# Attention scores as 64-row matmuls of two heads, and a listed order for TensorE, in a two-layer decoder trunk

## The chip, the cores and the metric

The kernel runs on one core of one Trainium2 chip. The metric is the time of one execution on the device in microseconds (us); lower is better. Before the change the median of three runs is 952.17 us (951.81 to 952.43). One execution was recorded by the hardware profiler; "the profile" and "the trace" mean that record. In it PE is TensorE's matmuls, PEld its weight loads, DVE VectorE, ACT ScalarE, POOL GpSimd and SP SyncE, which issues the DMAs.

## The reference

One sequence of 512 tokens, 1024 channels, goes through a pooling layer with its MLP, then an attention layer with its MLP. Keys and values are projected once, from the residual stream after the first layer. The attention has 16 heads of 64 channels:

```python
z = einsum('bhqd,bhkd->bhqk', q_blk, k_blk) / sqrt(64)      # strictly causal, s < t
log1m = where(mask, -softplus(z), 0)
excl = cumsum(log1m, reverse=True) - log1m                  # over the keys
a = where(mask, exp(log_sigmoid(z) + excl), 0)
o = einsum('bhqk,bhkd->bhqd', a, v_blk)
m = o.reshape(B, S, HD) @ w_o
x = x + rms_norm(m, mix_post_g)
```

In words: a weight is the sigmoid of its own score times the product of (1 − sigmoid) over the keys between it and the query. Everything is float32.

## The kernel before, in words

**Accuracy and products.** TensorE multiplies float32 in a rounded form (`F32R`). So operands are split: the high part is the value rounded by a copy on ACT, the low part the rest, by a subtraction on DVE. A full product is three matmuls, high x high, high x low and low x high (`mm3`, L300 to L302, and `up_block`, L708 to L712, for projections of q and k and the MLP's first matrix).

**Heads and pairs.** The 16 heads form 8 pairs. A projection gives one PSUM tile of 128 rows (partitions) x 512 tokens; its rows 0–63 are head 0 of the pair, rows 64–127 head 1. `queries_keys` (L931) makes from it, for each head `a` of the pair, operands of 128 rows: `k` holds the high part of the head's keys twice (own half and other half of the partitions), `kl` the low part in the own half and zeros in the other half (set once by POOL), `q` the high part of the queries in the own half and their low part in the other. With these, one matmul over 128 rows gives qh·kh + ql·kh, and a second one qh·kl (L991, L992): two products of 128 rows stand for the three of 64.

**Scores.** For a block `i` of 128 queries only the keys up to the block's end count: 128, 256, 384 or 512 of them. `scores` takes at least 256. Its results fill three PSUM banks per head: block 3, block 2, and blocks 1 and 0 together.

**Weights.** ACT takes two sigmoids of each bank: of −z (`against`, L1000) for the scan, and of z (`for_`, L1012). DVE runs one scan over all 1280 entries of a head (`scan`, L1016) and multiplies (`weigh`, L1022). The scan's result `e` has one buffer. Then TensorE transposes the weights (`turn`, L1035: 10 transposes a head, in three PSUM tiles), ACT and DVE split them (`high`, `low`, L1041, L1045), and `products` (L1052) multiplies them with the values; `out_low` and `out` (L1059, L1063) collect the pair's output.

**Values** are projected for four heads at a time (two pairs; `values`, L882), one block of 128 tokens after another, 24 matmuls of 256 columns each. A group holds two weight tiles until its last block is done. Output projections (`contract`, `projected`) follow in between.

**PSUM** is one pool of 8 banks of 128 x 512 float32; every score tile, projection, transpose tile and product takes one.

**Weights from memory.** The attention's weight matrices were split during the first MLP and written back in two parts (`kept`). Four slots in SBUF hold them; SP loads the next one when a slot comes free (`w<-kept`, L242).

**What orders the work.** `ATT_ORDER` lists the attention's steps. P is the q and k projections of a pair, S its scores and weights (up to `weigh`), T its transposes and their splits, A its products with the values, V a group of value projections with its token blocks, O an output projection, N and K the first transposes and the first half of the first key projection, E the last four pairs' output. Only up to the first P does `manual_schedule` fix TensorE's order as listed; behind that a planner orders all engines by its own model of their times. From the last step on, `END_ORDER` fixes the order of all engines by hand: there z is a score, x and y the two sigmoids, sc the scan, mu the weigh, T the transposes of the last pair, A, oc and od the products of the sixth and last pair, D and R loads, O, E, F and G output projections. In both lists the digits are a pair, a head, a block or a tile.

Of the kernel before, what the change touches and what calls it, by code (L numbers as in the profile page):

```python
# [10 lines left out]
F32 = mybir.dt.float32  # L11
F32R = mybir.dt.float32r
ACT = mybir.ActivationFunctionType
ALU = mybir.AluOpType

P = 128
# [16 lines left out]
TS = [slice(t * P, (t + 1) * P) for t in range(T)]  # L33
# [3 lines left out]
SEG = {3: (0, 512), 2: (512, 384), 1: (896, 256), 0: (1152, 128)}  # L37
# [20 lines left out]

ATT_ORDER = [
    (w[0], int(w[1]), [int(c) for c in w[2:]])  # L60
    for w in """V001 N2 K0 N3 V02 P0 V03 S0 P1 T0 V101 S1 A0 P2 T1 V123 A1 S2 P3 T2 O00123 A2 S3 P4 V201 T3 A3
    S4 P5 T4 V223 S5 A4 P6 V301 T5 S6 A5 V323 P7 T6 E1""".split()
]


# [5 lines left out]

END_ORDER = [
    (w if w.startswith("d7") else w.rstrip("0123456789"), [int(c) for c in w if c.isdigit() and not w.startswith("d7")])
    for w in """D6 R0 R1 z01 z00 x01 z02 x00 z11 x02 z12 y02 sc0 A60 y01 y00 x11 z10 oc60 A61 y11 x10 od60 E01 y10
    mu0 oc61 x12 E00 y12 od61 sc1 T00 hh6 T02 T01 ah00 O00 ah02 d7h ah01 O01 hl6 al02 F01 mu1 E11 ov01
    T11 al00 T10 ah11 al01 F11 ah10 al11 T12 A70 al10 ah12 d7l al12 ov00 A71 oc70 od70 O10 oc71 od71 F00
    ov10 hh7 O11 hl7 G01 ov11 G00 ev01 G11 ev00 s01 E10 ev11 s00 g01 s11 F10 V0 g00 G10 a01 O20 a00 S01
# [28 lines left out]
def trunk(ctx, tc, x, consts, grow, pw, wup, wdn, wq, wk, wv, wo, out):  # L106
    nc = tc.nc
    pool = lambda name, bufs=1, **kw: ctx.enter_context(tc.tile_pool(name=name, bufs=bufs, **kw))
# [10 lines left out]
    def name(s):  # L119
        uid[0] += 1  # L120
        return f"{s}{uid[0]}"

    def ps():
        return psum.tile([P, 512], F32, tag="ps", name=name("ps"))
# [29 lines left out]
    behind, latest = {}, {}  # L154
# [32 lines left out]
    def want(key, src, scaled=None):  # L187
        queue.append((key, src, scaled))
# [48 lines left out]
    def make():  # L237
        k, src, scaled = queue.pop(0)
        if k in kept:
            made[k] = place(k)  # L240
            for n, t in enumerate(made[k]):
                latest["sp"] = nc.sync.dma_start(t.bitcast(F32), kept[k][n])  # L242
            return
        made[k] = weight(src, place(k), scaled, dn_raw.pop(k, None))

    def fill(n=1):
        if gate[0]:
            behind.update(latest)
        for _ in range(n):
            if queue and len(made) < ahead and (queue[0][0][0] != "dn" or dn_pool[0]):  # L250
                make()
# [6 lines left out]
    for l in range(2):  # L258
        if l == 1:
            n = len(queue)  # L260
            for what, i, part in ATT_ORDER:
                if what == "V" and 0 in part:
                    for h in range(2):
                        want(("v", i, h), wv[i, h], gains(C_KV * KC + 4 * h, 4))
                elif what == "P":
                    want(("k", i), wk[i], gains(C_KV * KC, KC))
                    want(("q", i), wq[i], gains(C_MIX_PRE1 * KC, KC))
                elif what == "O" or what == "E":
                    for c in range(2 * i, 2 * i + 2 if what == "O" else PAIRS):
                        want(("o", c), wo[c])  # L270
            apart.extend(x for x in queue[n:] if x[0] not in [("o", c) for c in range(2)])

            queue[n - GRP : n + GRP] = queue[n : n + GRP] + queue[n - GRP : n]
        for j in range(NJ):
            want(("up", l, j), wup[l, j])
        for j in range(NJ - GRP, NJ):
            want(("dn", l, j), wdn[l, j])
# [442 lines left out]
    with tc.tile_pool(name="mix0", bufs=1, reuse_waits="tile") as mp:  # L720
# [29 lines left out]
        left, stats, ups, ys, own = {}, {}, {}, {}, {}  # L750
# [128 lines left out]
    with tc.tile_pool(name="att", bufs=1, reuse_waits="tile") as ap:  # L879
# [30 lines left out]
        def project(key):  # L910
            need(*range(T))
            if key in started:
                pq, w = started.pop(key)
                up_block(pq, w, slice(S // 2, S))
            else:
                pq = ps()
                up_block(pq, get(key), slice(0, S))
            return pq

        def qk_tile(tag):  # L920
            return ap.tile([P, S], F32R, tag=tag, name=name(tag))

        half = [slice(0, HD), slice(HD, P)]


        kls = [qk_tile(f"kl{a}") for a in range(2)]
        with tc.issue_after(latest["pool"].ins):
            for a in range(2):
                nc.gpsimd.memset(kls[a][half[1 - a], :].bitcast(F32), 0.0)

        def queries_keys(p):  # L931
            qs, ks = [], []
            pk = project(("k", p))
            for a in range(2):
                k, kl, own, other = qk_tile(f"k{a}"), kls[a], half[a], half[1 - a]
                nc.scalar.copy(k[own, :], pk[own, :])
                latest["act"] = nc.scalar.copy(k[other, :], pk[own, :])
                latest["dve"] = nc.vector.tensor_tensor(
                    out=kl[own, :], in0=pk[own, :], in1=k[own, :].bitcast(F32), op=ALU.subtract
                )  # L940
                ks.append(k)
            fill()
            pq = project(("q", p))
            for a in range(2):
                q, own, other = qk_tile(f"q{a}"), half[a], half[1 - a]
                latest["act"] = nc.scalar.copy(q[own, :], pq[own, :])
                latest["dve"] = nc.vector.tensor_tensor(
                    out=q[other, :], in0=pq[own, :], in1=q[own, :].bitcast(F32), op=ALU.subtract
                )
                qs.append(q)  # L950
            fill()
            return qs, ks

        begin = ap.tile([P, NSEG], mybir.dt.bfloat16, tag="begin", name="begin")
        us = [ap.tile([P, NSEG + 1], F32, tag=f"u{a}", name=f"u{a}") for a in range(2)]
        with tc.issue_after(latest["pool"].ins):
            nc.gpsimd.memset(begin, 0.0)  # L960
            for lo, n in SEG.values():
# [3 lines left out]
                    out=d, in_=d, pattern=[[-1, P + c]], base=c - 1, channel_multiplier=1,  # L965
# [6 lines left out]
        class Head:  # L972
# [9 lines left out]
                self.qk, self.p, self.a, self.u = qk, p, a, us[a]  # L982
                self.pz, self.pt, self.parts, self.to = {}, {}, {}, {}

            def scores(self, b):
                q, k, kl = self.qk[0][self.a], self.qk[1][self.a], kls[self.a]
                pz = self.pz[b] = ps()
                o = 0
                for i in self.SCORES[b][0]:
                    n = max(256, (i + 1) * P)  # L990
                    nc.tensor.matmul(pz[:, o : o + n], q[:, TS[i]], k[:, :n], start=True, stop=False)  # L991
                    nc.tensor.matmul(pz[:, o : o + n], q[:, TS[i]], kl[:, :n], start=False, stop=True)  # L992
                    o += n

            def against(self, b):
                tiles, at = self.SCORES[b]
# [64 lines left out]
            def out(self, o):  # L1061
                own = half[self.a]
                nc.vector.tensor_tensor(out=o[own, :], in0=self.po[half[0], :], in1=o[own, :], op=ALU.add)  # L1063

        def weights(p):
            hs = [Head(qk[p], p, a) for a in range(2)]
            for x in hs:
                for b in range(3):
                    x.scores(b)
                    x.against(b)  # L1070
                    x.for_(b)
                x.scan()
                x.weigh()
            return hs

        def transposed(hs):
# [25 lines left out]
        vs, os, wos, y = {}, {}, {}, y_tiles()  # L1102
# [6 lines left out]
        def end():  # L1109

            p, last = PAIRS - 2, PAIRS - 1
            heads[last] = [Head(qk[last], last, a) for a in range(2)]
            w = {c: get(("o", c)) for c in range(2, 6)}
            bank, o, ups, up, held = {}, {}, {}, {}, []
# [77 lines left out]
            def half_up(j):  # L1192
# [2 lines left out]

            last_heads = heads[last]
            steps = {
                "z": lambda a, b: last_heads[a].scores(b), "x": lambda a, b: last_heads[a].against(b),
                "y": lambda a, b: last_heads[a].for_(b), "sc": lambda a: last_heads[a].scan(),
                "mu": lambda a: last_heads[a].weigh(), "T": lambda a, b: last_heads[a].turn(b),  # L1200
                "ah": lambda a, b: last_heads[a].high(b), "al": lambda a, b: last_heads[a].low(b),
# [24 lines left out]
        qk, heads, gpost1 = {}, {}, None  # L1226

        def step(what, i, part):
            nonlocal gpost1
            if what == "V":  # L1230
                values(i, part)
            elif what == "N":
                need(i)
            elif what == "K":
                start(("k", i))
            elif what == "P":
                qk[i] = queries_keys(i)
                if i == PAIRS - 1:
                    until(("o", 5))
            elif what == "S":  # L1240
                gate[0] = True
                heads[i] = weights(i)
                fill()
            elif what == "T":
                transposed(heads[i])
                behind.update(latest)
            elif what == "A":
                mix_pair(i, vs[i // 2][1])
            elif what == "O" and part:
                out_proj(i, part)  # L1250
                if i == 0:
                    with tc.issue_after(latest["sp"].ins):
                        gpost1 = gain_row(R_MIX_POST1)

        first = [what for what, _, _ in ATT_ORDER].index("P") + 1
        with tc.manual_schedule(engines={mybir.EngineType.PE}):
            for x in ATT_ORDER[:first]:
                step(*x)
        for x in ATT_ORDER[first:-1]:
            step(*x)  # L1260
        end()


# [56 lines left out]
```

## Time and profile before

| | |
|---|---|
| runs | 951.81, 952.17, 952.43 us |
| the profiled execution | 952.24 us, of which span 950.5 us |
| TensorE busy | 940.9 us (99% of the span), 4758 matmuls |
| DVE, ACT busy | 707.9 and 577.8 us |
| TensorE's clock | 0.999 of full |
| the attention | about 362 to 611 us of the span |

A row of the order in time reads: start in us, length in us, engine, line, operation, output <- inputs, shape, count, and in brackets the idle time ahead of it with what ended it. A matmul's length contains its pipeline's depth and overlaps the next one, so the distance between starts is what it takes. A row that groups instructions by line has the count behind x, then busy us, mean ns of one, then idle time ahead of them and what ended it. A row of waits names who waited <- for whom, total us, times, longest. A row of a window has, behind the window and its length, the busy us and count of PE, PEld, DVE, ACT and POOL, then TensorE's clock, the DMA engines' share and GB/s.

### The profile page before, as it was taken

What the parts mean: (1) busy time and instruction counts of PE and PEld (TensorE: products, weight loads), DVE (VectorE), ACT (ScalarE), POOL (GpSimd) and SP (SyncE); (2) the same over time, 40 slices, a digit from 0 to 9 for tenths busy, and PEclk for the clock granted to TensorE, in tenths of its full rate; (3) what the DMA queues carried; (4) which work ended last, traced back from release to release, by engine and by line L of the source; (5) the groups of instructions that cost most, each with busy time, mean ns of one, the idle gap of its engine ahead of it and who ended that gap; (6) DMA issues with size and microseconds to landing.
All of it is one profiled execution on the core that took longest, in us unless ns stands there. A gap on an engine that the chain in (4) does not pass through costs nothing.

```text
span 950.5 us, 12510 instructions
## 1 busy us (share of the span) xinstructions
PE 940.9 (99%) x4758; PEld 799.7 (84%) x4758; DVE 707.9 (74%) x813; ACT 577.8 (61%) x1015; POOL 42.1 (4%) x85
## 2 busy tenths in 40 slices
PE   9999999999999999999999999999999999999996
PEld 7998888888888889899899988898888888888885
DVE  5875798988979976476577778874696966958756
ACT  6667979788775547456656554865545444444532
POOL 2300000000000004000000000200000000000002
PEclk9999999999999999999999999999999999999999
DMA  8244969789697760522424271442513233133102
GB/s 309 96 178 148 342 219 347 295 283 356 217 323 269 271 207 2 202 85 90 172 95 178 91 264 45 134 155 71 196 43 131 93 133 111 45 133 111 35 11 89
DMA packets 43262, 156.15 MB, mean 164 GB/s; under 512 B 4289, under 2 KB 4673, under 8 KB 43202
## 3 DMA queue, kind: packets, MB, share of 16 engines
q1 hardware_dynamic: 43202, 155.36, 46.1%
q8 instruction: 37, 0.61, 0.3%
q14 instruction: 23, 0.19, 0.1%
HBM read 121.79 MB, written 33.55 MB: 163 GB/s over the span
## 4 chain that ended last, share of the span: by engine, by line
PE 94%; DVE 2%; ACT 2%; POOL 1%; issue 1%; POOLq 0%; DVEq 0%; ACTq 0%
PE ps L589 28%; PE ps L708 15%; PE ps L712 15%; PE ps L711 15%; PE ps L300 4%; PE ps L301 4%; PE ps L302 4%; PE ps L1052 2%; PE ps L829 1%; PE ps L1035 1%; PE ps L991 1%; PE ps L395 1%; PE ps L992 1%; ACT xn L285 1%; PE ps L801 1%
## 5 line engine op out<-in xcount | busy, mean ns | idle before, releaser
L589 PE MATMUL ps<-w,a 128*128 128x512 f32 x1176 | 278.6, 389 | 0.0
L711 PE MATMUL ps<-xnh,w 128*128 128x512 f32 (+1 forms) x712 | 261.1, 369 | 0.0
L712 PE MATMUL ps<-xnl,w 128*128 128x512 f32 (+1 forms) x712 | 261.1, 368 | 0.0
L708 PE MATMUL ps<-xnh,w 128*128 128x512 f32 (+1 forms) x712 | 260.3, 368 | 0.1
L589 PEld LDWEIGHTS ps<-w,a 128*128 128x128 f32 x1176 | 220.7, 188 | 45.9 <-DVE w L282 0.2
L712 PEld LDWEIGHTS ps<-xnl,w 128*128 128x128 f32 x712 | 134.2, 189 | 21.8
L708 PEld LDWEIGHTS ps<-xnh,w 128*128 128x128 f32 x712 | 133.7, 189 | 22.4 <-DVE w L850 0.3
L711 PEld LDWEIGHTS ps<-xnh,w 128*128 128x128 f32 x712 | 133.8, 189 | 22.1
L598 DVE TENSOR_TENSOR y<-ps,y 128x512 f32<-128x512 f32 x124 | 84.5, 688 | 43.9 <-PE ps L589 43.7
L172 DVE TENSOR_TENSOR w<-raw,w 128x1024 fp32r<-128x1024 f32 x58 | 70.9, 1223 | 57.4 <-ACT w L170 57.2
L170 ACT CAST w<-raw 128x1024 fp32r<-128x1024 f32 x58 | 61.0, 1051 | 79.3 <-PE ps L708 79.2
L281 ACT CAST a<-r 128x768 fp32r<-128x768 f32 (+1 forms) x60 | 47.7, 794 | 72.1 <-PE ps L589 55.7
L282 DVE TENSOR_TENSOR a<-r,a 128x768 fp32r<-128x768 f32 (+1 forms) x60 | 54.1, 902 | 12.3 <-ACT a L281 12.1
L281 ACT CAST w<-e 128x1536 fp32r<-128x1536 f32 (+1 forms) x30 | 41.8, 1394 | 23.8 <-DVE e L563 14.4
L1016 DVE TENSOR_TENSOR_SCAN e<-u,begin 128x1280 f32<-128x1280 f32 x16 | 45.2, 2823 | 11.0 <-ACT u L1000 10.4
L282 DVE TENSOR_TENSOR w<-e,w 128x1536 fp32r<-128x1536 f32 (+1 forms) x30 | 49.5, 1649 | 1.8 <-ACT w L281 1.6
L181 ACT ACTIVATE apart<-apart,eye 128x128 f32<-128x128 f32 (+1 forms) x132 | 43.1, 407 | 0.5 <-DMA apart<-in_wk 0.5
L282 DVE TENSOR_TENSOR w<-w,w 128x1536 fp32r<-128x1536 f32 (+1 forms) x20 | 33.0, 1650 | 8.6 <-ACT w L281 8.6
L621 ACT ACTIVATE r<-ps 128x512 f32<-128x512 f32 x56 | 33.1, 591 | 8.6 <-PE ps L708 8.5
L282 DVE TENSOR_TENSOR w<-xn,w 128x1536 fp32r<-128x1536 f32 (+1 forms) x20 | 33.0, 1650 | 5.6 <-ACT w L281 5.5
L300 PE MATMUL ps<-w,xnh 128*128 128x256 f32 x128 | 36.6, 286 | 0.0
L622 ACT ACTIVATE r<-r 128x512 f32<-128x512 f32 x56 | 35.5, 634 | 1.3
(134 smaller groups left out, 1393.6 us busy)
## 6 DMA issues: line engine op xcount, KB each, us to landing
raw<-in_wup SPq DMA_DIRECT2D x64, 512.0 KB, 4.1
w<-kept SPq DMA_DIRECT2D x60, 512.0 KB, 4.2
kept<-wx SPq DMA_DIRECT2D x30, 512.0 KB, 5.0
w<-in_wdn SPq DMA_DIRECT2D x8, 1536.0 KB, 6.7
kept<-apart SPq DMA_DIRECT2D x24, 512.0 KB, 5.7
xn<-in_wdn SPq DMA_DIRECT2D x8, 1536.0 KB, 7.7
apart<-in_wk SPq DMA_DIRECT2D x7, 512.0 KB, 7.1
apart<-in_wq SPq DMA_DIRECT2D x7, 512.0 KB, 9.4
```

The source lines that it names most:

```text
L170: nc.scalar.copy(hi, raw)
L172: nc.vector.tensor_tensor(out=lo, in0=raw, in1=hi.bitcast(F32), op=ALU.subtract)
L181: nc.scalar.mul(c, c, gc[:, lo + k : lo + k + 1])
L281: latest["act"] = nc.scalar.copy(hi, src)
L282: latest["dve"] = nc.vector.tensor_tensor(out=lo, in0=src, in1=hi.bitcast(F32), op=ALU.subtract)
L300: nc.tensor.matmul(dst, ah, bh, start=start, stop=False)
L589: nc.tensor.matmul(bank, a[:, x, q, TS[t]], w[:, z, q], start=start and q == 0 and k == 0, stop=q == self.n - 1 and k == 2, skip_group_che ...
L598: nc.vector.tensor_tensor(out=part, in0=bank, in1=part, op=ALU.add)
L708: nc.tensor.matmul(pu[:, cols], wl[:, k, :], xnh[:, k, cols], start=False, stop=k == KC - 1)
L711: nc.tensor.matmul(pu[:, cols], wh[:, k, :], xnh[:, k, cols], start=k == 0, stop=False)
L712: nc.tensor.matmul(pu[:, cols], wh[:, k, :], xnl[:, k, cols], start=False, stop=False)
L1016: nc.vector.tensor_tensor_scan(out=self.e[:, ::-1], data0=self.u[:, 1:][:, ::-1], data1=begin[:, ::-1], initial=0.0, op0=ALU.mult, op1=ALU ...
```

## The change

The pair's keys and queries are kept as they come from the projection: one high and one low tile of 128 rows each, head 0 in the upper and head 1 in the lower half. The scores of a head are three matmuls over its own 64 rows, and the two heads' matmuls alternate, each into a bank of its own. The shortest block takes 128 columns and no longer 256. Copies and zeros that built the 128-row operands go. In `weights` all scores of a pair come first, then the sigmoids of −z of both heads, then the first head's scan, then the sigmoids of z. TensorE's order of the whole attention up to the last step is the listed one, and the list has the value projections one token block at a time where they were mostly two at a time; in the last part the six score steps of two heads become three of the pair, ahead of the sixth pair's products.

```diff
-    for w in """V001 N2 K0 N3 V02 P0 V03 S0 P1 T0 V101 S1 A0 P2 T1 V123 A1 S2 P3 T2 O00123 A2 S3 P4 V201 T3 A3
-    S4 P5 T4 V223 S5 A4 P6 V301 T5 S6 A5 V323 P7 T6 E1""".split()
+    for w in """V001 N2 K0 N3 V02 P0 V03 S0 P1 V10 T0 V11 S1 A0 P2 T1 V12 A1 V13 S2 P3 T2 O00123 A2 S3 P4 V201 T3 S4
+    A3 P5 V22 T4 V23 S5 A4 P6 V30 T5 V31 S6 A5 V323 P7 T6 E1""".split()
...
-    for w in """D6 R0 R1 z01 z00 x01 z02 x00 z11 x02 z12 y02 sc0 A60 y01 y00 x11 z10 oc60 A61 y11 x10 od60 E01 y10
+    for w in """D6 R0 R1 z1 z0 x01 z2 x00 x02 y02 sc0 A60 y01 y00 x11 oc60 A61 y11 x10 od60 E01 y10
...
-        kls = [qk_tile(f"kl{a}") for a in range(2)]
-        with tc.issue_after(latest["pool"].ins):
-            for a in range(2):
-                nc.gpsimd.memset(kls[a][half[1 - a], :].bitcast(F32), 0.0)
-
         def queries_keys(p):
-            qs, ks = [], []
-            pk = project(("k", p))
-            for a in range(2):
-                k, kl, own, other = qk_tile(f"k{a}"), kls[a], half[a], half[1 - a]
-                nc.scalar.copy(k[own, :], pk[own, :])
-                latest["act"] = nc.scalar.copy(k[other, :], pk[own, :])
-                latest["dve"] = nc.vector.tensor_tensor(
-                    out=kl[own, :], in0=pk[own, :], in1=k[own, :].bitcast(F32), op=ALU.subtract
-                )
-                ks.append(k)
-            fill()
-            pq = project(("q", p))
...
+            both = []
+            for what in "kq":
+                src = project((what, p))
+                hi, lo = qk_tile(f"{what}h"), qk_tile(f"{what}l")
+                latest["act"] = nc.scalar.copy(hi, src)
+                latest["dve"] = nc.vector.tensor_tensor(out=lo, in0=src, in1=hi.bitcast(F32), op=ALU.subtract)
+                both.append((hi, lo))
+                fill()
+            return both
...
-            def scores(self, b):
-                q, k, kl = self.qk[0][self.a], self.qk[1][self.a], kls[self.a]
-                pz = self.pz[b] = ps()
-                o = 0
-                for i in self.SCORES[b][0]:
-                    n = max(256, (i + 1) * P)
-                    nc.tensor.matmul(pz[:, o : o + n], q[:, TS[i]], k[:, :n], start=True, stop=False)
-                    nc.tensor.matmul(pz[:, o : o + n], q[:, TS[i]], kl[:, :n], start=False, stop=True)
-                    o += n
...
+        def scores(hs, b):
+
+
+            (kh, kl), (qh, ql) = hs[0].qk
+            for x in hs:
+                x.pz[b] = ps()
+            o = 0
+            for i in Head.SCORES[b][0]:
+                n = SEG[i][1]
+                for m, (x, y) in enumerate(((qh, kh), (qh, kl), (ql, kh))):
+                    for h in hs:
+                        own = half[h.a]
+                        nc.tensor.matmul(
+                            h.pz[b][:, o : o + n], x[own, TS[i]], y[own, :n], start=m == 0, stop=m == 2,
+                        )
+                o += n
+
         def weights(p):
             hs = [Head(qk[p], p, a) for a in range(2)]
+            for b in range(3):
+                scores(hs, b)
             for x in hs:
                 for b in range(3):
-                    x.scores(b)
                     x.against(b)
+            hs[0].scan()
+            for x in hs:
+                for b in range(3):
                     x.for_(b)
-                x.scan()
-                x.weigh()
+            hs[0].weigh()
+            hs[1].scan()
+            hs[1].weigh()
             return hs
...
-                "z": lambda a, b: last_heads[a].scores(b), "x": lambda a, b: last_heads[a].against(b),
+                "z": lambda b: scores(last_heads, b), "x": lambda a, b: last_heads[a].against(b),
...
-        first = [what for what, _, _ in ATT_ORDER].index("P") + 1
         with tc.manual_schedule(engines={mybir.EngineType.PE}):
-            for x in ATT_ORDER[:first]:
+            for x in ATT_ORDER[:-1]:
                 step(*x)
-        for x in ATT_ORDER[first:-1]:
-            step(*x)
         end()
```

More of the change, by code (lines that the diff above doesn't have):

```diff
@@ L267, in trunk @@
                     want(("q", i), wq[i], gains(C_MIX_PRE1 * KC, KC))
-                elif what == "O" or what == "E":
+                elif what == "O" and 0 in part or what == "E":
                     for c in range(2 * i, 2 * i + 2 if what == "O" else PAIRS):
@@ L923, in trunk @@
         half = [slice(0, HD), slice(HD, P)]
-        kls = [qk_tile(f"kl{a}") for a in range(2)]
-        with tc.issue_after(latest["pool"].ins):
-            for a in range(2):
-                nc.gpsimd.memset(kls[a][half[1 - a], :].bitcast(F32), 0.0)
         def queries_keys(p):
-            qs, ks = [], []
-            pk = project(("k", p))
-            for a in range(2):
-                k, kl, own, other = qk_tile(f"k{a}"), kls[a], half[a], half[1 - a]
-                nc.scalar.copy(k[own, :], pk[own, :])
-                latest["act"] = nc.scalar.copy(k[other, :], pk[own, :])
-                latest["dve"] = nc.vector.tensor_tensor(
-                    out=kl[own, :], in0=pk[own, :], in1=k[own, :].bitcast(F32), op=ALU.subtract
-                )
-                ks.append(k)
-            fill()
-            pq = project(("q", p))
[L944 to L952, printed above, removed]
+            both = []
[7 more added lines that the diff above has]
+            return both
         begin = ap.tile([P, NSEG], mybir.dt.bfloat16, tag="begin", name="begin")
@@ L1250, in step @@
                 out_proj(i, part)
-                if i == 0:
+                if gpost1 is None:
                     with tc.issue_after(latest["sp"].ins):
                         gpost1 = gain_row(R_MIX_POST1)
-        first = [what for what, _, _ in ATT_ORDER].index("P") + 1
         with tc.manual_schedule(engines={mybir.EngineType.PE}):
-            for x in ATT_ORDER[:first]:
+            for x in ATT_ORDER[:-1]:
                 step(*x)
-        for x in ATT_ORDER[first:-1]:
-            step(*x)
         end()
```

## The prediction

> **What bounds the kernel now.** I read the page's head and its chain first, then TensorE's waits, then one window over the attention, and last TensorE's rows in order of time.
>
> ```profile
> span 950.5 us, 12510 instructions
> PE 940.9 (99%) x4758; PEld 799.7 (84%) x4758; DVE 707.9 (74%) x813; ACT 577.8 (61%) x1015; POOL 42.1 (4%) x85
> ...
> PE 94%; DVE 2%; ACT 2%; POOL 1%; issue 1%; POOLq 0%; DVEq 0%; ACTq 0%
> ```
> ```profile
> PE ps L395 <- ACT xn L385: 0.5, 2, 0.3
> PE ps L991 <- DVE q L947: 0.4, 1, 0.4
> ```
> ```profile
> 362.00:611.00 249.00, 248.39 (x1475) 219.97 (x1474) 174.23 (x218) 148.01 (x333) 16.00 (x36) 1.00 0.35 127
> ```
> TensorE is the bound: 940.9 of 950.5 us, 94% of the chain, and full clock. In the attention (362 to 611 us, columns PE, PEld, DVE, ACT) it idles 0.6 us of 249, and of its waits only one of 0.4 us belongs to the lines that change. So the fixed order can recover almost nothing; a gain must come from fewer TensorE microseconds in the scores. DVE at 174 and ACT at 148 of 249 us have room.
>
> The busy time of a matmul row (0.39 us) overlaps its successor, so costs are read as distances between starts. The second pair's scores, and what surrounds another pair's:
>
> ```profile
> 414.30 0.39 PE L991 MATMUL ps<-k,q 128*128 128x512 f32 x1
> ...
> 414.77 0.34 PE L991 MATMUL ps<-k,q 128*128 128x384 f32 x1
> ...
> 415.11 0.28 PE L991 MATMUL ps<-k,q 128*128 128x256 f32 x1
> ...
> 415.59 0.40 PE L991 MATMUL ps<-k,q 128*128 128x512 f32 x1
> ...
> 416.87 0.40 PE L1052 MATMUL ps<-ah,v 128*128 128x512 f32 x1
> ```
> ```profile
> 395.47 0.40 PE L711 MATMUL ps<-xnh,w 128*128 128x512 f32 x1
> ...
> 406.37 2.35 PE L1035 MATMUL ps<-eye,w 128*128 128x128 f32 x20
> 408.47 0.36 PE L300 MATMUL ps<-w,xnh 128*128 128x256 f32 x1
> 408.68 0.28 PE L301 MATMUL ps<-w,xnh 128*128 128x256 f32 x1
> 408.80 0.28 PE L302 MATMUL ps<-w,xnl 128*128 128x256 f32 x1
> ```
> The reader sees: a pair's 16 score matmuls take 2.57 us (414.30 to 416.87); 48 projection matmuls of 512 columns take 10.90 us (395.47 to 406.37), 0.227 each, or 0.4435 ns a column; 384 columns take (415.11 − 414.77)/2 = 0.17, 256 columns (415.59 − 415.11)/4 = 0.12. Time follows columns. The 20 transposes (128 columns each) take 2.10 us, 0.105 each, although their columns are worth 0.057: there every matmul brings its own load of 128 columns, and I read 0.105 as the price of a load.
>
> **The change, part by part.**
>
> *Scores.* Removed: per pair 2 heads x 2 products x (512+384+256+256) columns, 16 matmuls. Added: 2 heads x 3 products x (512+384+256+128), 24 matmuls, each over 64 rows only; head 0 on partitions 0–63, head 1 on 64–127, alternating and into different PSUM banks. No row of this trace shows a 64-row matmul, so the price has two ends. Lower end: the two of a couple run side by side and cost one. Columns alone: 3 x 1280 x 0.4435 ns = 1.70 us; with 128 columns held at the load's 0.105, 3 x (0.227 + 0.17 + 0.12 + 0.105) = 1.87 us. Upper end: one after another, 3.73 us. I take the lower, because the nearest row is the 128-row matmul: in 0.227 us it streams 512 columns through the same two sets of partitions and writes one bank, and the couple reads the same partitions, each half once.
> The Trainium skill, page "TensorE: Matmul & The Clock Gate", section "Part 3: Packing small matmuls — row/col tiling", says that matmuls on different row groups run together and start about 4 ns apart; by it the couple costs one matmul; no row here shows it.
>
> *Edges.* TensorE goes into 64-row work and out again once per pair. The nearest row is another change of kind: after the last transpose the value projection's first matmul takes 408.68 − 408.47 = 0.21 where the next takes 0.12, so 0.09 more. The other end is an emptied pipe: the 0.39 us of a row less the 0.227 between starts, 0.163. I take 0.09 twice: 0.18 per pair, bounds 0 and 0.33.
> The Trainium skill, page "TensorEngine Tiling (Array Packing)", section "Key Properties", states that changing the tiling mode drains TensorE, which speaks against the change. If that is the full 0.163 each way, eight pairs pay 8 x 0.15 = 1.2 us more than I take and the sum below becomes 949.4.
>
> So a pair's scores go from 2.57 to 2.05 us: 0.52 saved, 7 pairs in the listed order: −3.6 us.
>
> *The last pair* is ordered apart, with the sixth pair's work.
>
> ```profile
> 561.63 2.35 PE L1035 MATMUL ps<-eye,w 128*128 128x128 f32 x20
> 563.73 0.42 PE L991 MATMUL ps<-k,q 128*128 128x384 f32 x1
> ...
> 565.70 0.41 PE L991 MATMUL ps<-k,q 128*128 128x384 f32 x1 [0.41 <-DVE q L947]
> ...
> 566.59 0.39 PE L1052 MATMUL ps<-ah,v 128*128 128x512 f32 x1
> ...
> 567.80 0.44 PE L991 MATMUL ps<-k,q 128*128 128x512 f32 x1
> ...
> 568.31 0.39 PE L1052 MATMUL ps<-ah,v 128*128 128x512 f32 x1
> ...
> 569.52 0.45 PE L300 MATMUL ps<-w,ohl 128*128 128x512 f32 x1
> ...
> 572.36 0.82 PE L1035 MATMUL ps<-eye,w 128*128 128x128 f32 x6
> ```
> ```profile
> 562.50 0.69 DVE L947 TENSOR_TENSOR q<-ps,q 64x512 fp32r<-64x512 f32 x1 [2.23 <-ACT q L946]
> 563.22 1.62 DVE L1045 TENSOR_TENSOR al<-ps,ah 128x512 fp32r<-128x512 f32 x3
> 564.87 0.69 DVE L947 TENSOR_TENSOR q<-ps,q 64x512 fp32r<-64x512 f32 x1
> 565.59 1.62 DVE L1045 TENSOR_TENSOR al<-ps,ah 128x512 fp32r<-128x512 f32 x3
> ...
> 570.44 1.48 DVE L1022 TENSOR_TENSOR w<-w,e 128x1280 f32<-128x1280 f32 x1
> ```
> From the scores' start to the last pair's own transposes TensorE needs 572.36 − 563.73 = 8.63 us now, with a wait of 0.41 for the second half of q. After: 2.05 + two P·V blocks of 1.21 (566.59 to 567.80, 568.31 to 569.52) + 2.84 of output projection (569.52 to 572.36) = 7.31. The second half of q no longer comes late; late next is a bank: six score banks are now asked for right behind six transpose banks, and the fourth of those comes free at about 565.4 (first three lows end at 564.84, then one more 0.55). Its user, the last couple of banks, would be reached 1.4 us into the scores, at about 565.1, so I add 0.3: 7.6, a gain of 1.0. The transposes then want the weigh (ends 571.92 now) at 571.35; DVE has one q row of 0.69 less ahead of it, so it ends at 571.23. Just in time.
>
> *ACT and DVE.* Per pair six ACT copies of 64x512 become two of 128x512, and four DVE subtractions become two:
>
> ```profile
> L936 ACT CAST k<-ps 64x512 fp32r<-64x512 f32 x16 | 9.3, 582 | 27.9 <-DVE kl L938 16.3 <-PE ps L708 11.5
> L947 DVE TENSOR_TENSOR q<-ps,q 64x512 fp32r<-64x512 f32 x16 | 11.0, 688 | 7.5 <-ACT q L946 7.2
> ```
> That frees 4 x 0.58 and 2 x 0.69 us per pair, off the path: worth nothing by itself. The two memsets on POOL that go have no one waiting.
>
> *Fixed order.* Before, only the first pair's part was listed for TensorE; the planner then chose nearly the same order as the new list has (scores, next projections, transposes). What a fixed list can cost is a transpose that waits for its weights. The narrowest place is the third pair, where only the next pair's 48 projection matmuls lie between:
>
> ```profile
> 440.80 0.45 PE L991 MATMUL ps<-k,q 128*128 128x512 f32 x1
> ...
> 454.31 2.35 PE L1035 MATMUL ps<-eye,w 128*128 128x128 f32 x20
> ```
> ```profile
> 443.94 2.83 DVE L1016 TENSOR_TENSOR_SCAN e<-u,begin 128x1280 f32<-128x1280 f32 x1 [1.64 <-ACT u L1000]
> ...
> 447.26 1.48 DVE L1022 TENSOR_TENSOR w<-w,e 128x1280 f32<-128x1280 f32 x1
> ...
> 449.80 2.82 DVE L1016 TENSOR_TENSOR_SCAN e<-u,begin 128x1280 f32<-128x1280 f32 x1
> ...
> 453.12 1.47 DVE L1022 TENSOR_TENSOR w<-w,e 128x1280 f32<-128x1280 f32 x1
> ```
> The second head's weigh ends at 454.59 and its transposes start at 454.31 + 1.05 = 455.36: 0.77 us of cover. After, they start 0.52 earlier; the first scan can start some 0.3 earlier too, since the sigmoids that feed it now go ahead of the others on ACT. Cover left: about 0.5. If it is gone, TensorE pays what DVE is late. The fifth pair's scores now follow the fourth's transposes directly: the bank wait of the last pair again, 0.3 to 0.4. I allow 0.6 for both.
>
> *Value projections by quarters* keep their 24 matmuls each. Only one of them moves past something that matters: the second group's last quarter now stands behind the P·V block, so the weight slot that it frees is refilled later.
>
> ```profile
> 438.47 0.80 SPq L242 DMA_DIRECT2D w<-kept  x2
> ```
> ```profile
> w<-kept SPq DMA_DIRECT2D x60, 512.0 KB, 4.2
> ```
> These two loads are the q weights of the fourth pair, issued when that value block lets its slot go; they are wanted after the scores and the key half of the next projection, 2.05 + 5.45 = 7.5 us against 4.2 to land. Hidden; the queue behind them on SP carries loads wanted later still.
>
> **Sum.** −3.6 − 1.0 + 0.6 = −4.0 us, against the profiled execution's 952.24 (span 950.5 and 1.74 around it; it stands 0.07 above the median 952.17): **948.2**. Lower bound: 1.70 per pair without edges or waits, 7 x −0.87 and −1.35 in the last: 944.8.
>
> **The rivals.**
>
> *Loads in line.* Side by side the matmuls, but the two heads' loads follow each other. Then a couple costs at least 2 x 0.105: 3 x (0.227 + 3 x 0.21) = 2.57 + 0.18 = 2.75 us, 0.18 above before: 7 x 0.18, −0.3 in the last pair, +0.6: 953.8. With 0.12 a load and edges of 0.33 the pair takes 3.21: 957. For it: the transposes at 0.105 show loads that do not overlap each other; against: those are all of 128 rows. It decides from 2.6 us a pair.
>
> *No sharing at all* (the change does not do what it says): 3.73 + 0.18 = 3.91 per pair, +1.34 x 7, +0.8 in the last, +0.6: 963.0. For it: nowhere in this trace do two matmuls share the array; against: nothing but the disjoint halves.
>
> *Transposes wait.* The fixed list leaves TensorE at the second head's transposes while DVE is still at its scan: price 2.83 us where a scan slips behind one other DVE row of that size, or 0.6 to 1 us at each of seven. It turns the sign from 4.6 us in all; with 6 us it gives 953.6. For it: cover of 0.77 before; against: DVE and ACT lose work and the planner still orders both.
>
> **How the numbers follow.** Chances: forecast 0.54, loads in line 0.20, no sharing 0.10, transposes wait 0.16. A change under 0.2% (1.9 us) is about what a measurement of this kernel cannot tell from none. The forecast lies beyond it but for a strip (0.52 faster, 0.02 same); loads in line and waiting transposes split between same (0.13) and slower (0.23); no sharing is slower. So faster 0.52, same 0.15, slower 0.33. The range leaves out no sharing and the tails: 945 to 957; the forecast's own is 945 to 950.
>
> **What would show it.** Right: the score matmuls come 24 to a pair with 2.0 to 2.2 us from first to next block, couples at almost equal starts; TensorE's waits in 362 to 611 us stay under 1.5 us; no L947-like wait in the last pair. Wrong: pairs at 2.6 or more with load rows 0.105 apart (loads in line), 0.227 between the two of a couple (no sharing), or PE waits on DVE's weigh ahead of transposes. All else, before 362 and after 611, should keep its length.

## The result, and the profile after

The changed kernel takes 949.35 us (median of 8 runs, 949.06 to 949.62); the kernel before, run beside it, 951.97 us (8 runs, 951.63 to 952.43). The ratio is 0.9972 with a 95% interval of 0.9962 to 0.9982: 2.6 us faster, where 4.0 were forecast. The profiled execution of the changed kernel took 949.25 us.

The head of its page, its row for 362 to 611 us (window and length, then busy us and count of PE, PEld, DVE, ACT, POOL), and TensorE's waits:

```profile
span 947.4 us, 12570 instructions
PE 938.1 (99%) x4822; PEld 796.4 (84%) x4822; DVE 696.0 (73%) x797; ACT 559.1 (59%) x983; POOL 41.2 (4%) x83
```
```profile
362.00:611.00 249.00, 248.69 (x1561) 219.22 (x1560) 164.24 (x205) 132.19 (x308) 15.19 (x35) 1.00 0.36 127
```
```profile
PE ps L395 <- ACT xn L385: 0.5, 2, 0.3
...
PE ps L1006 <- ACT ah L1012: 0.2, 1, 0.2
```

TensorE is still the bound. It has 64 matmuls more and is busy 2.8 us less; ACT lost 16 us and DVE 10 in this window, of which 0.3 us at most came back in the time ("The list alone", below).

The span moves by some tenths of a microsecond from run to run outside the attention, so from here on I compare one length (pairs are counted from one: the third pair is 2 in the lists): from the first value projection (L300 on `xnh`, 256 columns) to the first matmul of the second MLP (L711, 256 columns). Before, and then after:

```profile
368.46 0.28 PE L300 MATMUL ps<-w,xnh 128*128 128x256 f32 x1
...
610.08 0.28 PE L711 MATMUL ps<-xnh,w 128*128 128x256 f32 x1
```
```profile
368.10 0.28 PE L300 MATMUL ps<-w,xnh 128*128 128x256 f32 x1
...
607.10 0.28 PE L711 MATMUL ps<-xnh,w 128*128 128x256 f32 x1
```

That is 241.62 and 239.00 us: the 2.62 us between them are the whole gain. A second profile of the changed kernel gave 239.01. Cut into blocks, each from its first matmul's start to the next block's:

| blocks | before | after | difference |
|---|---|---|---|
| scores, 8 pairs | 21.57 | 16.82 | −4.75 |
| products with the values (A) | 20.07 | 20.68 | +0.61 |
| projections of q and k (P) | 87.78 | 88.16 | +0.38 |
| value projections (V) | 46.36 | 46.91 | +0.55 |
| transposes (T) | 16.64 | 17.36 | +0.72 |
| output projections | 45.90 | 45.75 | −0.15 |

The scores paid what was expected of them. Nearly half of it was given back in the blocks around them, whose own work had not changed. Of the transposes' 0.72, 0.34 is a wait at the third pair's ("ACT in the written order", below) and 0.35 stands ahead of the fifth and the last pair's scores, which follow transposes directly (blocks of 2.28 and 2.27 us instead of 2.10). Where the rest went, the second pair's rows show (TensorE's matmuls in order of time, changed kernel; x2 is one matmul of each head):

```profile
413.39 0.28 PE L301 MATMUL ps<-w,xnh 128*128 128x256 f32 x1
413.51 0.28 PE L302 MATMUL ps<-w,xnl 128*128 128x256 f32 x1
413.72 0.50 PE L1048 MATMUL ps<-kh,qh 64*128 64x512 f32 x2
414.05 0.39 PE L1048 MATMUL ps<-kl,qh 64*128 64x512 f32 x2
414.29 0.40 PE L1048 MATMUL ps<-kh,ql 64*128 64x512 f32 x2
414.52 0.33 PE L1048 MATMUL ps<-kh,qh 64*128 64x384 f32 x2
...
415.57 0.27 PE L1048 MATMUL ps<-kh,ql 64*128 64x128 f32 x2
415.77 0.50 PE L1023 MATMUL ps<-ah,v 128*128 128x512 f32 x1
416.11 0.40 PE L1023 MATMUL ps<-al,v 128*128 128x512 f32 x1
416.35 0.33 PE L1023 MATMUL ps<-ah,v 128*128 128x384 f32 x1
```

The couples run side by side: 0.24 and 0.23 us from one couple of 512 columns to the next, what a single matmul took. The whole pair takes 2.05 us (413.72 to 415.77). But the way in costs on both of its sides: the last matmul before it 0.21 instead of 0.12 (413.51 to 413.72), and the first couple 0.33 instead of 0.23. So does the way out: the last couple 0.20 where 128 columns take about 0.11, and the first matmul behind it 0.34 instead of 0.23. That is about 0.2 each way, half of it outside the scores.

The weight loads (PEld, same place) of the two heads go side by side too, two in the 0.19 us of one, and at the way in the load that otherwise runs 0.12 us after the last one comes only after 0.33:

```profile
413.39 0.19 PEld L302 LDWEIGHTS ps<-w,xnl 128*128 128x128 f32 x1
413.72 0.19 PEld L1048 LDWEIGHTS ps<-kh,qh 64*128 64x128 f32 x2
```

### The profile page after: what moved, and what is told of

It is laid out like the page before. It is cut to its first block, busy times and chain, and to the rows that moved or that the text cites. A ratio compares the mean times of both kernels' runs of the same rounds, so it can differ in the third digit from the quotient of the medians.

```text
span 947.4 us, 12570 instructions
## 1 busy us (share of the span) xinstructions
PE 938.1 (99%) x4822; PEld 796.4 (84%) x4822; DVE 696.0 (73%) x797; ACT 559.1 (59%) x983; POOL 41.2 (4%) x83
## 4 chain that ended last, share of the span: by engine, by line
PE 94%; DVE 1%; ACT 1%; POOL 1%; DMA 1%; issue 1%; SPq 0%; POOLq 0%; DVEq 0%; ACTq 0%
PE ps L589 28%; PE ps L711 15%; PE ps L708 15%; PE ps L712 15%; PE ps L300 4%; PE ps L302 4%; PE ps L301 4%; PE ps L1023 2%; PE ps L1048 2%; PE ps L1006 2%; PE ps L829 1%; PE ps L395 1%; ACT xn L285 1%; DMA band<-in_consts 1%; PE ps L801 1%; POOL stat L296 1%
## 5 line engine op out<-in xcount | busy, mean ns | idle before, releaser
L711 PE MATMUL ps<-xnh,w 128*128 128x512 f32 (+1 forms) x712 | 261.6, 369 | 0.0
L711 PEld LDWEIGHTS ps<-xnh,w 128*128 128x128 f32 x712 | 133.9, 189 | 22.1
L300 PE MATMUL ps<-w,xnh 128*128 128x256 f32 x128 | 36.7, 287 | 0.0
```

Of the source, the lines that this page charges most:

```text
L300: nc.tensor.matmul(dst, ah, bh, start=start, stop=False)
L711: nc.tensor.matmul(pu[:, cols], wh[:, k, :], xnh[:, k, cols], start=k == 0, stop=False)
```

## The experiments

Each difference is in the attention's length as just defined, unless a run's time is named; times are medians, with the ratio to the kernel before run beside them.

**The list alone.** The kernel before, with the new list:

```diff
-        for x in ATT_ORDER[first:-1]:
-            step(*x)
+        with tc.manual_schedule(engines={mybir.EngineType.PE}):
+            for x in ATT_ORDER[:-1]:
+                step(*x)
```

> The kernel before with the new list for TensorE up to the last step (quarters of the value projections, scores of the fifth pair directly behind the fourth's transposes), its scores still of 128 rows. Theory (the 64-row blocks themselves lengthen their neighbours, the list costs next to nothing): 0 to +0.6 us against before, TensorE's blocks of P, A and V as long as before. Rival (the list and the quarters cost the 2.1 us that the blocks around the scores lost): +1.5 to +2.1 us, with P, A and V blocks 0.09 longer as in the changed kernel.

952.05 us, ratio 1.0001 (0.9992 to 1.001); length 241.81, +0.19. Its blocks are A 20.06, P 87.82, V 46.43: as before the change. So what A, P and V lost in the changed kernel is not the list's or the quarters' doing. The rival is out.

The 0.19 lie in the output projection behind the third pair's transposes. It takes 11.77 us here and 11.60 before the change, and in both a matmul comes late; here the profile names DVE's low parts (L1045):

```profile
457.47 0.50 PE L300 MATMUL ps<-w,ohl 128*128 128x512 f32 x1 [0.22 <-DVE al L1045]
```

Before the change the same matmul comes 0.44 us after the one ahead of it (457.66 to 458.10); in the changed kernel it is 0.23 (456.70 to 456.93), and the block takes 11.29:

```profile
457.66 0.40 PE L302 MATMUL ps<-w,ohl 128*128 128x512 f32 x1
458.10 0.50 PE L300 MATMUL ps<-w,ohl 128*128 128x512 f32 x1
```
```profile
456.70 0.40 PE L302 MATMUL ps<-w,ohl 128*128 128x512 f32 x1
456.93 0.39 PE L300 MATMUL ps<-w,ohl 128*128 128x512 f32 x1
```

So 0.31 us of the gain is a wait for DVE that went. The likely reason is that DVE has fewer rows of q and k ahead of those low parts; no run separates it.

**The 64-row scores alone.** The changed kernel with the old list and the planner behind the first projection:

> The changed kernel with the old list, fixed for TensorE only up to the first projection, so that the planner orders the rest; the scores are of 64 rows. It plans the same blocks, but cuts the fifth pair's scores into six pieces among the fourth pair's products. Theory (each way into and out of 64-row work costs about 0.19 us): five more ways in and out, 1.9 us, and three cut couples of 0.2 more, 1.5 to 2.5 us above the changed kernel. Rival (edges are free): within 0.5 us of it.

956.55 us, ratio 1.0049 (1.0035 to 1.0063); 7.2 us above the changed kernel's median, far more than expected. The profiled execution was one of the longer ones (958.08), its length 247.59, 8.6 above. The cut scores of the fifth pair are 3.65 us of it (scores +2.64, products +1.01). Most of the rest, 3.4 us, is a wait that I had not expected here, the second head's transposes of the third pair:

```profile
454.09 1.25 PE L1006 MATMUL ps<-eye,w 128*128 128x128 f32 x10
...
457.96 2.37 PE L1006 MATMUL ps<-eye,w 128*128 128x128 f32 x10 [2.61 <-DVE w L993]
```

Those weights come late because the planner puts other work ahead of them: ACT does two other casts (443.94 and 444.45) among the third pair's sigmoids, so the first scan starts 5.5 us after the first of them (442.02 to 447.54; 4.1 in the changed kernel), and DVE splits another weight tile (455.21) ahead of the second head's weigh. By itself the list is worth nothing; beside the 64-row scores the old order costs more than the scores win. This run undoes the quarters as well, so the parts of the list were not told apart.

**One matmul between the scores, and its control.** A 128-row matmul of 512 columns in each of seven pairs, once between the second and the third step (`b == 2`), once ahead of the first (`b == 0`):

```diff
             for x in hs:
                 x.pz[b] = ps()
+            if b == 2 and hs[0].p < PAIRS - 1:
+                nc.tensor.matmul(hs[0].pz[b], xnh[:, 0, TS[0]], xnh[:, 0, :], start=True, stop=True)
```

> The changed kernel with one more matmul in each of the seven listed pairs: 128 rows, 512 columns, into the bank that the next scores overwrite, between the second and the third step of the scores, so that TensorE leaves 64-row work and comes back once more. Theory (each way in or out costs about 0.19 us): 0.23 + 0.38 = 0.61 us a pair, +4.2 us on the changed kernel, and +2.6 on the run with the same matmul ahead of the scores. Rival (what the neighbours lose belongs to the list or to ACT and DVE): +1.6 us, the same as the matmul ahead.

> The control: the same extra matmul of 128 rows and 512 columns in the same seven pairs, ahead of the scores, beside other 128-row work, so no more ways in or out. Both theories: 7 x 0.23 = +1.6 us on the changed kernel.

Inside: 953.19 us, ratio 1.0013 (1.0004 to 1.0021); ahead: 951.05 us, 0.9988 (0.9980 to 0.9997). In the attention the control adds 1.67 us, as both theories had it, and the matmul inside 3.90. In the control the border moves with the matmul: the value projections that stood ahead of the scores are shorter again (2.87 us for 2.96 at the first pair), and the extra matmul, now the scores' neighbour, takes 0.32 instead of 0.23. The inside run has 0.35 us less of waiting at transposes than the changed kernel (its T blocks sum to 17.01); without that it is 3.90 + 0.35 − 1.59 = 2.66 us for seven ways out and back, 0.38 each. The rows of the inside run:

```profile
415.34 0.34 PE L1050 MATMUL ps<-kl,qh 64*128 64x384 f32 x2
415.52 0.34 PE L1050 MATMUL ps<-kh,ql 64*128 64x384 f32 x2
415.79 0.50 PE L1043 MATMUL ps<-xnh 128*128 128x512 f32 x1
416.22 0.39 PE L1050 MATMUL ps<-kh,qh 64*128 64x256 f32 x2
416.44 0.28 PE L1050 MATMUL ps<-kl,qh 64*128 64x256 f32 x2
416.56 0.28 PE L1050 MATMUL ps<-kh,ql 64*128 64x256 f32 x2
```

The lone matmul holds 0.43 us (415.79 to 416.22) instead of 0.23, the couple ahead of it 0.27 instead of 0.17, the couple behind 0.22 instead of 0.12. The price of a change between 128 and 64 rows is shown: 0.19 us each way, on both sides of it.

**Which neighbours share.** First the inner loops swapped, so that head 0's three products of a block come ahead of head 1's three:

```diff
-                for m, (x, y) in enumerate(((qh, kh), (qh, kl), (ql, kh))):
-                    for h in hs:
-                        own = half[h.a]
+                for h in hs:
+                    own = half[h.a]
+                    for m, (x, y) in enumerate(((qh, kh), (qh, kl), (ql, kh))):
```

> The changed kernel with the two inner loops of the scores swapped: for each block all three products of head 0, then all three of head 1, the same 24 matmuls. Theory (two matmuls on different halves run side by side when they are neighbours in the order, and TensorE starts them in order): only the neighbours at the seams overlap, four instead of three times a block's length, 0.62 us more a pair, +4 to +6 us on the changed kernel. Rival 1 (the halves are independent queues, the order among them does not matter): +-0.5 us. Rival 2 (only matmuls that read the same columns share): one after another, 1.9 us more a pair, +13 to +15 us.

948.53 us, ratio 0.9963 (0.9949 to 0.9976). My theory falls. The couples form all the same:

```profile
413.31 0.51 PE L1048 MATMUL ps<-kh,qh 64*128 64x512 f32 x2
413.64 0.41 PE L1048 MATMUL ps<-kl,qh 64*128 64x512 f32 x2
413.87 0.40 PE L1048 MATMUL ps<-kh,ql 64*128 64x512 f32 x2
```

Head 1's first matmul is now the fourth in the list, and it starts beside the first, ahead of the second and third (two overtaken). The two halves are fed as two streams, across the order of the list. (The length is 0.42 below the changed kernel's, 0.34 of it the wait at the third pair's transposes, which does not occur here.) How far the look ahead reaches, the next run shows: all twelve matmuls of head 0 ahead of all twelve of head 1 (`scores` then takes the heads as an argument, not shown).

```diff
-            for b in range(3):
-                scores(hs, b)
+            for a in range(2):
+                for b in range(3):
+                    scores(hs, b, (a,))
```

> The changed kernel with all twelve score matmuls of head 0 listed ahead of all twelve of head 1 (three banks, then three). Theory (each half of the rows is a stream of its own and TensorE looks far ahead): 2.06 us a pair as before, within 0.5 us of the changed kernel; the first head's sigmoids get no earlier scores. Rival (it looks ahead only past the three matmuls that a swapped inner loop asked for): the second head's matmuls start late, up to 1.5 us more a pair, +5 to +12 us.

960.10 us, ratio 1.0085 (1.0071 to 1.0099); a pair's scores take 3.63 us instead of 2.06. The second pair, in order of time (the row with x2 at 417.20 is head 1's first block of 512 columns and, with the same name and operands, head 0's last block):

```profile
415.63 0.49 PE L1047 MATMUL ps<-kh,qh 64*128 64x512 f32 x1
415.97 0.39 PE L1047 MATMUL ps<-kl,qh 64*128 64x512 f32 x1
...
417.19 0.28 PE L1047 MATMUL ps<-kh,ql 64*128 64x256 f32 x1
417.20 0.50 PE L1047 MATMUL ps<-kh,qh 64*128 64x512 f32 x2
417.37 0.28 PE L1047 MATMUL ps<-kl,qh 64*128 64x128 f32 x1
417.48 0.27 PE L1047 MATMUL ps<-kh,ql 64*128 64x128 f32 x1
417.54 0.39 PE L1047 MATMUL ps<-kl,qh 64*128 64x512 f32 x1
```

Head 1's first matmul, thirteenth in the list, starts beside the ninth (417.20 and 417.19), ahead of the tenth, eleventh and twelfth: it overtakes three matmuls and no more, in each of the seven listed pairs alike, where the swapped loops needed two. The first eight ran alone. A wait for a bank is unlikely: the changed kernel writes its fourth bank 0.80 us after a pair's first matmul (414.52 − 413.72), here it is 1.57 (417.20 − 415.63).

**ACT in the written order.** In `weights` the sigmoids of −z stand first, but the planner, which still orders ACT, had alternated them with those of z, and the first scan of the third pair started at 445.00, 5.07 us after its scores began (439.93), where before the change it was 3.14. The changed kernel there: DVE's rows, then TensorE's, the start of the scores and the two runs of ten transposes, of which the second comes 0.3 late:

```profile
445.00 2.82 DVE L987 TENSOR_TENSOR_SCAN e<-u,begin 128x1280 f32<-128x1280 f32 x1 [3.39 <-ACT u L971]
...
452.78 1.48 DVE L993 TENSOR_TENSOR w<-w,e 128x1280 f32<-128x1280 f32 x1
```
```profile
439.93 0.50 PE L1048 MATMUL ps<-kh,qh 64*128 64x512 f32 x2
...
453.00 1.25 PE L1006 MATMUL ps<-eye,w 128*128 128x128 f32 x10
454.41 1.28 PE L1006 MATMUL ps<-eye,w 128*128 128x128 f32 x10 [0.15 <-ACT ah L1012]
```
```diff
+            def after_last(f, b):
+                with tc.issue_after(latest["act"].ins):
+                    latest["act"] = f(b)
+
             for x in hs:
                 for b in range(3):
-                    x.against(b)
+                    after_last(x.against, b)
```

(and the same for `for_`; both functions then return their last instruction).

> The changed kernel with ACT held to the order in which the sigmoids are written down (all of -z of both heads, then all of z); the planner had alternated them. Theory (the second head's weigh of the third pair came 0.3 us late because the first scan started 5.1 us after its scores): the scan starts about 2 us earlier, TensorE's wait at those transposes goes, -0.3 us, all else as it was. Rival (that wait comes from the bank or from ACT's copies of the transposes): 0.

948.68 us, ratio 0.9967 (0.9955 to 0.9980). The length is 238.65, −0.35, and the 20 transposes of the third pair are one run of 2.10 us again. The scan starts 2.74 us after the scores (443.23 − 440.49):

```profile
440.49 0.50 PE L1049 MATMUL ps<-kh,qh 64*128 64x512 f32 x2
```
```profile
443.23 2.83 DVE L988 TENSOR_TENSOR_SCAN e<-u,begin 128x1280 f32<-128x1280 f32 x1 [1.80 <-ACT u L971]
```

The wait was the late scan's, though the profile's label names ACT's `ah`.

**The shortest block.** The changed kernel with 256 columns, and the kernel before with 128:

```diff
-                n = SEG[i][1]
+                n = max(256, SEG[i][1])
```
```diff
-                    n = max(256, (i + 1) * P)
+                    n = (i + 1) * P
```

> The changed kernel with the shortest block of scores at 256 columns again, as before the change (the 128 more are computed and never read). Theory (128-row and 64-row matmuls of 256 columns take 0.12, of 128 columns 0.06 to 0.11): three couples, 0.1 us a pair, +0.8 us on the changed kernel. Rival (loads bound the short ones at 0.105 anyway): +0.3 us.

> The kernel before with the shortest block of scores at 128 columns, nothing else changed: how much of the gain needs no 64-row matmul. Four short matmuls a pair. Theory (two matmuls of 128 columns took 0.17 us together in the P.V products, of 256 columns 0.24): -0.14 us a pair, -1.1 us against before. Rival (loads bound them at 0.105): -0.5 us.

With 256: 949.91 us, 0.9976 (0.9966 to 0.9985), length +0.49, between the theory's 0.8 and the rival's 0.3; the scores take 0.07 us a pair more, which decides for neither. Before with 128: 952.06 us, 0.9997 (0.9988 to 1.0006), length −0.12: neither my theory's 1.1 us are there nor the rival's 0.5. The rows tell why (kernel before with 128, last two matmuls of head 0, then head 1):

```profile
415.55 0.22 PE L991 MATMUL ps<-k,q 128*128 128x128 f32 x1
415.61 0.28 PE L992 MATMUL ps<-kl,q 128*128 128x128 f32 x1
415.72 0.45 PE L991 MATMUL ps<-k,q 128*128 128x512 f32 x1
416.01 0.39 PE L992 MATMUL ps<-kl,q 128*128 128x512 f32 x1
```

The two short ones take 0.17 instead of 0.24, and the matmul behind them 0.29 instead of 0.23. What is won is handed to the neighbour. So before the change the short block was worth nothing. In the changed kernel about 0.5 of the 2.6 us hang on it; the other 2.1 do not need it, and they need the sharing, since without it (heads apart, above) the kernel is slower than before.

**A version with both waits removed.** The changed kernel, ACT in the written order, and value projections moved between transposes and scores: first `V20 T3 V21 S4` for `V201 T3 S4`, then also `V32 P7 T6 V33` for `V323 P7 T6`.

> The changed kernel itself, on the chip of the next three, to compare with. 949.1 to 949.7 us.

> The changed kernel with ACT held to the written order of the sigmoids, and one value projection moved between the fourth pair's transposes and the fifth pair's scores. Theory: the wait of 0.3 at the third pair's transposes goes, the way in from transposes (0.18 and 0.07 more in the scores) becomes the ordinary one, -0.5 us on the changed kernel. Rival (ways in cost the same from anywhere): -0.3.

> The same, and the last value projection moved between the sixth pair's transposes (seventh in counting from one) and the last pair's scores. Theory: the last pair's bank wait of 0.2 and the dearer way in go too, -0.8 us on the changed kernel. Rival (the value weights hold two slots 2.9 us longer, and the output weights that take them land late): a new TensorE wait on a DMA in the last part, 0.5 us or more slower than the run before it.

On one chip: the changed kernel 949.24 us, ratio 0.9971 (0.9960 to 0.9983); the first version 949.07, 0.9970 (0.9958 to 0.9982); the second 948.71, 0.9965 (0.9953 to 0.9978). The lengths are 239.01, 238.57 and 238.41. The moved projections bring 0.08 and 0.16 on top of ACT's order. My theory had 0.2 for the first: the way in costs nearly the same from transposes as from elsewhere, closer to the rival. Both together give 0.60 where 0.8 was expected, and the feared wait on output weights did not come. The second version has no TensorE wait left at the scores or at the listed pairs' transposes, but the last pair's transposes wait 0.24 us for DVE's weigh (0.14 in the changed kernel, see below). It beats the kernel before; that it beats the changed kernel, 0.5 us, is in the trace but inside the intervals of the times.

## Why the prediction was right, and where it was not

*What bounds the kernel*: right. Matmul time in the scores passed into the whole, less what the borders took; the freed ACT and DVE time did not, but for the 0.31 us behind the third pair's transposes.

*Scores*: right in mechanism and size. I had chosen the lower end, couples side by side with loads that follow the columns, 1.87 us and 2.05 with edges; 2.05 to 2.07 were measured in six of the seven listed pairs, 2.14 in the fifth. The Trainium skill's "Part 3" of "TensorE: Matmul & The Clock Gate" was borne out that matmuls on different row groups run together (0.23 us a couple of 512 columns, as a single one); that matmuls start strictly in program order, as it also has it, was not (fourth beside first, thirteenth beside ninth).

*Edges*: the term that was mis-sized. I took 0.09 each way from the row after the transposes, 0.18 a pair, with 0.33 as the outer bound. The runs with one matmul inside gave 0.38. My 0.09 is the delay of one side; a second, as long, falls on the matmul across the border, so it does not show in the scores' own length, and I looked only there. Eight pairs x 0.20 = 1.6 us more than I took. The table has 1.5 in A, P and V and 0.35 in T, of which 0.1 is the list's (P and V in the run of the list alone). The Trainium skill's rule that changing the tiling mode drains TensorE ("TensorEngine Tiling (Array Packing)", "Key Properties") agrees with these rows; even the drain that I worked out for it, 0.163, was too small beside 0.19. The 949.4 that I had by that rule lies 0.05 from the measured time; that is partly luck, since other terms were off in both directions.

*The last pair*, from its scores to its own transposes:

```profile
561.46 0.45 PE L1048 MATMUL ps<-kh,qh 64*128 64x384 f32 x2
...
568.98 0.40 PE L302 MATMUL ps<-w,ohl 128*128 128x512 f32 x1
569.35 1.28 PE L1006 MATMUL ps<-eye,w 128*128 128x128 f32 x10
```

These are 7.89 us, where I had 7.6 and 8.63 were before: 0.74 won for 1.0. The wait for a bank is there about as worked out (scores 2.30 instead of 2.07; I had 0.3). What is missing lies behind them: products and output blocks take 5.59 instead of 5.26 us. Of that, 0.14 is a wait that I had ruled out as "just in time": the last output matmul holds 0.37 us (568.98 to 569.35) instead of 0.23, because the weigh ends only at 569.20 (DVE, 567.73 + 1.47). The other 0.18 is in the products, with the way out of the scores.

*Fixed order*: 0.6 allowed, 0.34 at the third pair's transposes and 0.07 in the fifth pair's scores found, and wrong in one reason. I let the first scan start 0.3 us earlier because the sigmoids that feed it are written first; the planner did not keep the written order, it started 1.9 later, and the cover of 0.5 us became a wait of 0.34.

*Value projections by quarters* at nothing: right within 0.1 us. *ACT and DVE* at nothing: 0.31 us too little.

*The rivals*: loads in line and no sharing are both disproved by the rows of the changed kernel. Transposes wait: 0.34 us at the third pair and 0.14 at the last, far from the 4.6 at which it would have decided. Under the planner's order that rival would have come near: there such waits and the cut scores make the 64-row scores 4.5 us slower than the kernel before.

The lower bound of 944.8 says without waits but keeps the last pair's 0.3 (without it, 944.5); nothing hangs on it.

So 4.0 were forecast and 2.6 came. The other half of the edges cost about 1.7 us, the list's 0.1 included, and the last pair 0.26 more than forecast; against them stand 0.26 of the 0.6 allowed for waits that was not used, the 0.31 won behind the third pair's transposes, and 0.1 more from the scores.

## What to carry to other kernels

Two heads of 64 channels can have their scores for the price of one if their matmuls lie in different halves of the rows, write different banks (not varied here), and stand no more than three places apart in TensorE's order; twelve places were too far. Count 0.38 us for each stretch of such work and look for its price in the neighbours as well, so make the stretches few and never cut them. Check what order the other engines really got: where a planner still arranges ACT and DVE, the written order of the sigmoids says nothing about when the scan starts.

## What the runs showed of the hardware that I had not expected

A 64-row matmul started ahead of up to three matmuls that stood before it in the list, if they used the other half of the rows (fourth beside first with the loops swapped; thirteenth beside ninth with the heads apart, 3.63 us a pair against 2.06). Of two loads of 64 rows each, both start together (413.72, x2). A change between 128-row and 64-row work takes 0.19 us, split between the last matmul on the one side and the first on the other. Shortening 128-row matmuls from 256 to 128 columns next to long ones gained 0.07 us a couple and lost 0.06 on the next.
